# A hybrid decoder trunk on one core: a joined block merge, narrower state-space taps, parameters and a mask moved

## The chip, the cores and the metric

The kernel runs on one core of a Trainium2 chip. The metric is device time in microseconds (us) of one execution. Engines: TensorE (PE, matmuls; PEld is its weight load), VectorE (DVE), ScalarE (ACT), GpSimd (POOL), and SyncE (SP), whose queue issues all DMAs here.

## What is computed

Two layers over 512 tokens of width 1024, batch 1. Layer 0 mixes with gated DeltaNet heads (4 heads of 128, chunked) and dilated sliding-window attention (8 heads of 64); layer 1 with a diagonal complex state-space mixer (S5: 64 groups of 16 channels, 64 states). Each mixer is followed by cross attention into 256 memory tokens and a SwiGLU feed-forward part, with post-norm after each. The parts that the change touches, cut from the reference:

```python
decay = jnp.exp(jnp.where(causal, g[..., :, None] - g[..., None, :], -jnp.inf))
lower = jnp.where(strict, jnp.einsum('bhnid,bhnjd->bhnij', k_beta, k), 0.0) * decay
sol = lax.linalg.triangular_solve(lower + eye, rhs, left_side=True, lower=True, unit_diagonal=True)
...
a_bar = jnp.exp(a * dt)
b_bar = ((a_bar - 1.0) / a)[..., None] * lax.complex(b_re.astype(f32), b_im.astype(f32))
_, states = lax.associative_scan(_lin_rec_combine, (a_seq, bu), axis=1)
y = (jnp.einsum('ghp,bsgp->bsgh', c_re, states.real) - jnp.einsum('ghp,bsgp->bsgh', c_im, states.imag))
```

## The kernel before

**Work.** Large products are made of three matmuls on high and low halves: ACT rounds a loaded weight tile (`raw`) to `hi`, DVE subtracts to make `lo` (`_load`, lines 504 to 516), PE multiplies. There are two `raw` buffers and four each of `hi` and `lo`. Small products use f32 operands directly.

**Order.** The program isn't issued as written. Each call adds an operation to a list (`Order.add`); `Order.order` (line 283) then plays the list through with a cost for each operation and a latency between engines, and always gives a free engine the ready operation of lowest priority number. The number is the place in the program plus `bias`; weights come 200 places early, and `LATER` = 100 puts an operation 100 places later. Limits on tile buffers keep it from running far ahead. The result is a fixed order on each engine's queue. `together` puts several matmuls side by side as one planned operation. The cost function has no entry for loading an ACT function table.

**Stages.** `build` (line 1624): mixer 0, output projection and norm, values of the memory, cross attention (`xattn`), feed-forward part 0 with the state-space tables as fill, state-space mixer, its gated output, cross attention, feed-forward part 1.

**Mixer 0** (line 600). Constants come first: `upper`, `masks`, a 64 KB `level` mask and the 640 KB attention mask (lines 632 and 633, in one `big` tile), convolution weights and small parameters, then the weights of the beta and decay logits. After the key projection, 16 matmuls of the broadcast log decay `gl` with the triangular `upper` give every row's cumulated decay (line 770). For the triangular solve the unit lower blocks are inverted by levels. Sixteen (head, chunk) matrices of 128 hold four 32x32 blocks each; all 64 are inverted on DVE in 31 steps (two operations a step, line 826 on). Line 844 then adds `s5_params` to the list: small DVE operations on 128x32 tiles, with Sin and Tanh on ACT, that make `rot`, `rho4`, `cin`, `cout` for the tables. The gate projection z follows (line 853). The 32x32 inverses are laid out block-diagonally (`Xm`, and transposed in `TTs`), and each chunk is merged to 64x64 blocks (lines 867 to 883): the lower coupling is masked by `level`, and three products of four full 128x128x128 f32 matmuls follow; both copies are updated by a subtraction. The merge to 128 (lines 884 to 896) uses 64x64x64 matmuls on one quadrant. The recurrence over chunks, then the attention follow.

**Tables** (`s5_tables`, line 1327). For each of 8 blocks of 8 groups the taps are made: for q in 4, a matmul with a 128x128 stationary slice of `st` and a 32-column moving slice of `cb`, real and imaginary part accumulated (lines 1467 to 1470), one ACT copy, the skip weight on the diagonal, and copies into a banded matrix that is stored to DRAM (`s5m`) and read in the state-space stage. Every block is one step of the fill of feed-forward part 0, at `LATER`.

Of the kernel before, what the change touches and what calls it, by code (L numbers as in the profile page):

```python
# [12 lines left out]
AF = mybir.ActivationFunctionType  # L13
OP = mybir.AluOpType
AX = mybir.AxisListType

P = 128
# [3 lines left out]
NT = S // P  # L21
# [17 lines left out]
LATER = 100  # L39
# [416 lines left out]
def run(steps):  # L456
    for _ in steps:
        pass


class Trunk:
# [23 lines left out]
    def t2(self, dt=F32):  # L485
        return self.o.tile(self.tp, [P, 512], dt, self.nm("t2"), "t2", T2)
# [113 lines left out]
    def mixer0(self, fill):  # L600
        tc, nc, a = self.tc, self.nc, self.a
        V, A, G, T = self.o.V, self.o.A, self.o.G, self.o.T
        sb = self.cp
        t2, tiny = self.t2, self.tiny
        small = lambda w, name="s", dt=F32: sb.tile([P, w], dt, name=self.nm(name), bufs=1)
        w_in = a["hyb_w_in"][0]

        xTv, _, actf, actt = self.feat_view([self.big() for _ in range(4)])
# [14 lines left out]
        upper = small(P, "upper")  # L623
# [4 lines left out]
        ktok = self.big(F32).rearrange("p (t c) -> p t c", t=4)  # L628
        cb = self.big(F32)
        attm = cb[:, :1280]  # L630
        level = cb[:, 1280:1408]
        self.o.SP.dma_start(level, a["level"])
        self.o.SP.dma_start(attm, a["attmask"])
        convw = small(48, "convw")
        self.o.SP.dma_start(convw, a["conv_t"])
        prm = small(8, "prm")
# [69 lines left out]
        gl = small(16, "gl")  # L706
# [3 lines left out]
        gc = small(16, "gc")  # L710
# [50 lines left out]
        LTs, Ds = four(), four()  # L761
        hsl = lambda h: slice(h * P, (h + 1) * P)
        h4 = lambda x: x.rearrange("p (h c) -> p h c", h=4)
        bc4 = lambda m: m[:, None, :].to_broadcast([P, 4, P])
        for c in range(NT):
            gB = self.bank()
            Dc = Ds[:, c]
            for h in range(4):
                o = c * 4 + h
                T.matmul(gB[:, hsl(h)], gl[:, o:o + 1].to_broadcast([P, P]), upper, start=True, stop=True)  # L770
            for h in range(4):
                o = c * 4 + h
                V.scalar_tensor_tensor(Dc[:, hsl(h)], gB[:, hsl(h)], gc[:, o:o + 1], causal, op0=OP.subtract, op1=OP.min)
            A.activation(Dc, Dc, AF.Exp)
# [15 lines left out]
        for c in range(NT):  # L790
            ts = slice(c * P, (c + 1) * P)
            rB = self.bank()
            gr = self.bank()
            for h in range(4):
                o = c * 4 + h
# [3 lines left out]
            for h in range(4):  # L799
                o = c * 4 + h  # L800
# [8 lines left out]
        TTs = four()  # L809
# [24 lines left out]
        for c in range(NT):  # L834
            ts = slice(c * P, (c + 1) * P)
# [3 lines left out]
            for h in range(4):  # L839
                o = c * 4 + h  # L840
                Dh = Ds[:, c, hsl(h)]
                V.scalar_tensor_tensor(Dh, qk[:, hsl(h)], rk[:, o:o + 1], Dh, op0=OP.mult, op1=OP.mult)

        self.s5_params()


        def z_sink(tt, ps):
            th = t2()
# [1 line left out]
            V.scalar_tensor_tensor(th, th, 1.0, ps, op0=OP.add, op1=OP.mult)  # L850
            V.scalar_tensor_tensor(h4(zgt[:, tt]), h4(th), 0.5, bc4(normg), op0=OP.mult, op1=OP.mult)

        self.gemm_tok(w_in, 0, KT, 1536, actt, NT, z_sink, tail=TAIL)


# [2 lines left out]
        Xms = []  # L858
        for c in range(NT):
            self.o.SP.dma_start(Xc[:, c], s2v[c])  # L860
            Xm = t2()
            V.tensor_tensor(Xm.rearrange("p (h b i) -> p h b i", h=4, b=4), Xc[:, c, :, None, :].to_broadcast([P, 4, 4, 32]),
                            bm[:, None, :, None].to_broadcast([P, 4, 4, 32]), op=OP.mult)
            tp = self.transposes(lambda h: Xm[:, hsl(h)], 4)
            A.activation(TTs[:, c], tp, AF.Copy)
            Xms.append(Xm)
        for c in range(NT):
            XT, Xm = TTs[:, c], Xms[c]
            E = t2()
            V.tensor_tensor(h4(E), h4(LTs[:, c]), bc4(level), op=OP.mult)  # L870
            yp = self.bank()
            for h in range(4):
                T.matmul(yp[:, hsl(h)], E[:, hsl(h)], Xm[:, hsl(h)], start=True, stop=True)
            Y = t2()
            A.activation(Y, yp, AF.Copy)
            xp = self.bank()
            for h in range(4):
                T.matmul(xp[:, hsl(h)], XT[:, hsl(h)], Y[:, hsl(h)], start=True, stop=True)
            xtp = self.bank()
            for h in range(4):  # L880
                T.matmul(xtp[:, hsl(h)], Y[:, hsl(h)], XT[:, hsl(h)], start=True, stop=True)
            V.tensor_tensor(Xm, Xm, xp, op=OP.subtract)
            V.tensor_tensor(XT, XT, xtp, op=OP.subtract)
        lo_, up_ = slice(0, 64), slice(64, P)
        for c in range(NT):
            LT, XT, Xm = (h4(x) for x in (LTs[:, c], TTs[:, c], Xms[c]))
            yp = self.bank()
            for h in range(4):
                T.matmul(h4(yp)[up_, h, lo_], LT[lo_, h, up_], Xm[lo_, h, lo_], start=True, stop=True)
            Y = t2()  # L890
            A.activation(h4(Y)[up_, :, lo_], h4(yp)[up_, :, lo_], AF.Copy)
            xtp = self.bank()
            for h in range(4):
                T.matmul(h4(xtp)[lo_, h, up_], h4(Y)[up_, h, lo_], XT[up_, h, up_], start=True, stop=True)
            V.tensor_scalar(XT[lo_, :, up_], h4(xtp)[lo_, :, up_], -1.0, None, op0=OP.mult)
# [16 lines left out]
        for c in range(NT):  # L912
            ts = slice(c * P, (c + 1) * P)
            Dc, TT = Ds[:, c], TTs[:, c]
            vb = vbt[:, c]
            if c:
# [4 lines left out]
                for h in range(4):  # L921
                    o = c * 4 + h
                    V.scalar_tensor_tensor(r[:, hsl(h)], kS[:, hsl(h)], nrbg[:, o:o + 1], vb[:, hsl(h)],
                                           op0=OP.mult, op1=OP.add)
# [7 lines left out]
            if c < NT - 1:  # L932
# [4 lines left out]
                if c:  # L937
                    for h in range(4):
                        V.scalar_tensor_tensor(Sn[:, hsl(h)], St[:, hsl(h)], egl[:, c * 4 + h:c * 4 + h + 1], su[:, hsl(h)],
                                               op0=OP.mult, op1=OP.add)  # L940
# [6 lines left out]
            if c:  # L947
# [4 lines left out]
                for h in range(4):  # L952
                    V.scalar_tensor_tensor(o_[:, hsl(h)], qS[:, hsl(h)], eg[:, c * 4 + h:c * 4 + h + 1], o_[:, hsl(h)],
                                           op0=OP.mult, op1=OP.add)
# [17 lines left out]
            for h in range(4):  # L972
                V.scalar_tensor_tensor(om[:, hsl(h)], o_[:, hsl(h)], ms[:, h:h + 1], zgt[:, c, hsl(h)],
                                       op0=OP.mult, op1=OP.mult)
# [352 lines left out]
    def s5_tables(self):  # L1327

        a = self.a
        V, A, G, T = self.o.V, self.o.A, self.o.G, self.o.T  # L1330
# [71 lines left out]
        for b in range(8):  # L1402
# [6 lines left out]
            blk = lambda n: part(n).rearrange("p (q c) -> p q c", q=4)  # L1409
            st = [self.t2() for _ in range(2)]  # L1410
# [47 lines left out]
            for n in range(2):  # L1458
                tp = self.transposes(lambda k: st[n][:, k * P:(k + 1) * P], 4)
                A.activation(part(2 + n), tp, AF.Copy)  # L1460

            cb = self.t2()
            cbv = cb[:, :256].rearrange("p (n q g h) -> p n q g h", n=2, q=4, g=2)
            for n in range(2):
                V.tensor_tensor(cbv[:, n], C[n][:, qs, None, :].to_broadcast([P, 4, 2, 16]),
                                self.gmask[:, n, None, :, None].to_broadcast([P, 4, 2, 16]), op=OP.mult)
            tp = self.bank()
            for q in range(4):
                for n in range(2):
                    T.matmul(tp[:, q * 32:(q + 1) * 32], st[n][:, q * P:(q + 1) * P],  # L1470
                             cb[:, n * P + q * 32:n * P + q * 32 + 32], start=(n == 0), stop=(n == 1))
            ts = self.t2()
            tsv = ts[:, :P].rearrange("p (q c) -> p q c", q=4)
            A.activation(ts[:, :P], tp[:, :P], AF.Copy)
            di = ts[:, P:2 * P].rearrange("p (q c) -> p q c", q=4)
            V.tensor_tensor(di[96:], self.ident[96:, None, 96:].to_broadcast([32, 4, 32]),
# [2 lines left out]
            for d in range(4):  # L1479
                src = tsv[(3 - d) * 32:(4 - d) * 32]  # L1480
                for k in range(4 - d):
                    dst = blk(6)[k * 32:(k + 1) * 32, :, (k + d) * 32:(k + d + 1) * 32]
# [141 lines left out]
    def build(self):  # L1624
        self.setup()
        k = self.mem_k(0)
        self.mixer0(k)
        run(k)
        self.mix_out0()
        run(self.mem_v(0))  # L1630
        self.xattn(0)
        tables = self.s5_tables()
        self.hp, self.hp_open = [self.big(F32) for _ in range(2)], True
        self.ffn(0, None, tables)
        self.hp_open = False
        run(tables)
        kv = chain(self.mem_k(1), self.mem_v(1))
        for _ in range(PRE):
            next(kv)
        gtok = self.s5(kv)  # L1640
        self.glu(gtok)
        self.xattn(1)
        self.ffn(1, self.to_out())
        self.o.issue()
# [58 lines left out]
```

## Time and profile before

| | us |
|---|---|
| median of 3 runs | 1561.4 (1559.45 to 1561.63) |
| the profiled execution | 1559.76 |
| its span, first to last instruction | 1557.9 |
| PE busy | 1523.2 |
| DVE busy | 989.4 |
| ACT busy | 555.2 |

Nearly every instruction carries line 439, the helper that issues the planned list, so groups are told apart by tile and shape. `big`, `t`, `tiny`, `ps` stand for all tiles of a pool. A line of a timeline has the start, the time from start to end of the merged run, engine, line, operation, out<-in, shape, count, and in brackets the idle time before it with what ended it. An f32 matmul appears as two records, a transpose through PE as one.

### The profile page before, as it was taken

To read this page: it belongs to the slowest core of one execution; us is meant where nothing else is said; L and a number is where in the kernel's file an instruction comes from. 1 tells how busy PE (TensorE), PEld (TensorE's weight loads), DVE (VectorE), ACT (ScalarE), POOL (GpSimd) and SP (SyncE) were. 2 spreads that over 40 slices of the span, in tenths; PEclk is the share of its full clock that TensorE was granted. 3 is DMA by queue.
4 is the path that set the end of the run, shared out by engine and by line. 5 is a ranking of instruction groups with operands and counts; after the bars stand their busy time and mean duration, and the time that the engine had idled before them with its cause. 6 is when DMAs were issued, how large, how long until landed. Compare 5 with 4: busy or idle time off the path is not lost.

```text
span 1557.9 us, 20944 instructions
## 1 busy us (share of the span) xinstructions
PE 1523.2 (98%) x8132; PEld 1285.8 (83%) x8132; DVE 989.4 (64%) x1890; ACT 555.2 (36%) x996; POOL 57.6 (4%) x97
## 2 busy tenths in 40 slices
PE   7999999999999999999999899999999999999998
PEld 5887878689888888888888798888888888888886
DVE  6989666675657788635853899648647444234436
ACT  6533436624432343323441243323422332122311
POOL 1000000010100000010000000000000000000000
PEclk9999999999999999999999999999999999999999
DMA  6423224135213454436572553333212433233322
GB/s 180 123 70 96 82 81 136 60 99 154 81 62 115 122 187 143 172 117 196 196 234 86 213 174 136 115 114 103 75 55 82 122 96 95 82 108 105 98 68 95
DMA packets 125539, 184.06 MB, mean 118 GB/s; under 512 B 14144, under 2 KB 84800, under 8 KB 121344
## 3 DMA queue, kind: packets, MB, share of 16 engines
q1 hardware_dynamic: 125440, 182.73, 37.3%
q8 instruction: 64, 1.05, 0.3%
q14 instruction: 35, 0.29, 0.1%
HBM read 162.52 MB, written 20.19 MB: 117 GB/s over the span
## 4 chain that ended last, share of the span: by engine, by line
PE 84%; DVE 10%; DMA 2%; ACT 2%; issue 1%; SPq 0%; POOL 0%; DVEq 0%; ACTq 0%; POOLq 0%
PE ps L439 83%; DVE t L439 5%; DVE big L439 2%; DVE lo L439 2%; PE ps L437 1%; DMA raw<-in_xo_w_dram 1%; ACT big L439 1%; DVE tiny L439 1%; ACT hi L439 1%; DMA big<-s5m 0%; ACT L439 0%; DMA t<-in_x_t_dram 0%; DMA raw<-in_xv_w_dram 0%; DMA raw<-in_hyb_w_in_dram 0%; DMA prm<-in_dn_a_log_dram 0%
## 5 line engine op out<-in xcount | busy, mean ns | idle before, releaser
L439 PE MATMUL ps<-big,hi 128*128 128x512 f32 (+1 forms) x2368 | 648.3, 360 | 6.0 <-ACT hi L439 4.5
L439 PE MATMUL ps<-hi,big 128*128 128x512 f32 x1728 | 547.8, 394 | 0.7 <-ACT big L439 0.4
L439 PEld LDWEIGHTS ps<-big,hi 128*128 128x128 f32 x2368 | 419.8, 189 | 69.8 <-ACT hi L439 5.0
L439 ACT ACTIVATE hi<-raw 128x1024 fp32r<-128x1024 f32 (+2 forms) x252 | 263.4, 1046 | 517.5 <-PE ps L439 341.9
L439 DVE TENSOR_TENSOR lo<-raw,hi 128x1024 fp32r<-128x1024 f32 (+2 forms) x252 | 303.5, 1205 | 226.2 <-ACT hi L439 223.9
L439 PE MATMUL ps<-big,lo 128*128 128x512 f32 (+1 forms) x1184 | 424.1, 360 | 2.4 <-DVE lo L439 2.4
L439 PEld LDWEIGHTS ps<-hi,big 128*128 128x128 f32 x1728 | 322.5, 188 | 66.1 <-DVE big L439 0.9
L439 PE MATMUL ps<-lo,big 128*128 128x512 f32 x864 | 339.1, 394 | 4.2 <-DVE lo L439 3.9
L439 PEld LDWEIGHTS ps<-big,lo 128*128 128x128 f32 x1184 | 223.8, 189 | 34.0 <-DVE lo L439 3.0
L439 PEld LDWEIGHTS ps<-lo,big 128*128 128x128 f32 x864 | 162.4, 188 | 39.3 <-DVE lo L439 6.6
L439 ACT ACTIVATE big<-ps 128x256 fp32r<-128x256 f32 (+2 forms) x188 | 89.6, 508 | 205.8 <-PE ps L439 196.9
L439 ACT ACTIVATE t<-ps 128x512 f32<-128x512 f32 (+4 forms) x133 | 66.7, 512 | 155.7 <-PE ps L439 151.3
L439 DVE TENSOR_TENSOR big<-ps,big 128x256 fp32r<-128x256 f32 (+1 forms) x152 | 77.5, 541 | 54.6 <-ACT big L439 52.6
L439 DVE SCALAR_TENSOR_TENSOR big<-big,ps 128x512 f32<-128x512 f32 x56 | 38.3, 684 | 93.8 <-PE ps L439 93.8
L439 DVE SCALAR_TENSOR_TENSOR t<-t,ps 128x512 f32<-128x512 f32 x72 | 48.9, 681 | 56.7 <-ACT t L439 51.7
L439 ACT ACTIVATE big<-t 32x128 f32<-32x128 f32 (+2 forms) x148 | 64.4, 455 | 32.4 <-DVE t L439 14.2
L439 DVE SCALAR_TENSOR_TENSOR big<-big,tiny,t 128x512 f32<-128x512 f32 x96 | 66.5, 744 | 0.0
L439 PE MATMUL ps<-ident,t 128*128 128x128 f32 x336 | 61.1, 276 | 4.7 <-ACT t L439 3.0
L439 POOL TENSOR_TENSOR tiny<-tiny,mhalf 128x1 f32<-128x1 f32 (+1 forms) x28 | 23.6, 846 | 965.8 <-DVE tiny L439 965.8
L439 PEld LDWEIGHTS ps<-ident,t 128*128 128x128 f32 x336 | 41.8, 141 | 16.4 <-issue 5.6
L439 PE MATMUL ps<-big,big 128*128 128x256 f32 (+2 forms) x328 | 55.2, 314 | 0.0
L439 DVE TENSOR_TENSOR big<-t,big 128x512 fp32r<-128x512 f32 (+1 forms) x68 | 44.0, 680 | 13.9 <-ACT big L439 13.7
(144 smaller groups left out, 994.4 us busy)
## 6 DMA issues: line engine op xcount, KB each, us to landing
raw<-in_ffn_wg_dram SPq DMA_DIRECT2D x44, 512.0 KB, 3.6
raw<-in_ffn_wu_dram SPq DMA_DIRECT2D x44, 512.0 KB, 3.7
raw<-in_ffn_wd_dram SPq DMA_DIRECT2D x44, 512.0 KB, 3.8
s5m<-big SPq DMA_DIRECT2D x16, 1024.0 KB, 4.5
big<-s5m SPq DMA_DIRECT2D x16, 1024.0 KB, 5.1
raw<-in_hyb_w_in_dram SPq DMA_DIRECT2D x26, 512.0 KB, 3.6
raw<-in_xk_w_dram SPq DMA_DIRECT2D x16, 512.0 KB, 4.8
raw<-in_xv_w_dram SPq DMA_DIRECT2D x16, 512.0 KB, 3.8
```

The costliest lines, as they stand in the source:

```text
L437: op.inst = getattr(self.eng[e], f)(*a, **k)
L439: op.inst = getattr(self.eng[e], fn)(*args, **kw)
```

## The change

Five edits. (1) The `level` load goes, and the attention mask is fetched just ahead of the gate projection. (2) The rows of cumulated decay come from a transpose of the broadcast `gc` instead of a matmul with `upper`. (3) The merge from 32 to 64 works on the 32x32 blocks themselves, for all 16 matrices at once: three stages of 16 pairs, each pair one 32x32x32 matmul for either 64-row half, into one bank a stage, without the mask; the results are copied into place with the sign turned. (4) The taps' operands are exchanged: `cb` slices of 32 columns are stationary, `st` moves, the four q go to four column groups of one bank; the result is copied and transposed once. (5) `s5_params` is called between the memory values and the first cross attention, with `LATER`.

```diff
@@ mixer0
-        level = cb[:, 1280:1408]
-        self.o.SP.dma_start(level, a["level"])
-        self.o.SP.dma_start(attm, a["attmask"])
...
-                T.matmul(gB[:, hsl(h)], gl[:, o:o + 1].to_broadcast([P, P]), upper, start=True, stop=True)
+                T.transpose(gB[:, hsl(h)], gc[:, o:o + 1].to_broadcast([P, P]), self.ident)
...
-        self.s5_params()
...
+        self.o.SP.dma_start(attm, a["attmask"])
         self.gemm_tok(w_in, 0, KT, 1536, actt, NT, z_sink, tail=TAIL)
...
-        for c in range(NT):
-            XT, Xm = TTs[:, c], Xms[c]
-            E = t2()
-            V.tensor_tensor(h4(E), h4(LTs[:, c]), bc4(level), op=OP.mult)
-            yp = self.bank()
-            for h in range(4):
-                T.matmul(yp[:, hsl(h)], E[:, hsl(h)], Xm[:, hsl(h)], start=True, stop=True)
-            Y = t2()
-            A.activation(Y, yp, AF.Copy)
-            xp = self.bank()
-            for h in range(4):
-                T.matmul(xp[:, hsl(h)], XT[:, hsl(h)], Y[:, hsl(h)], start=True, stop=True)
-            xtp = self.bank()
-            for h in range(4):
-                T.matmul(xtp[:, hsl(h)], Y[:, hsl(h)], XT[:, hsl(h)], start=True, stop=True)
-            V.tensor_tensor(Xm, Xm, xp, op=OP.subtract)
-            V.tensor_tensor(XT, XT, xtp, op=OP.subtract)
+        blk = [(slice(g * 64, g * 64 + 32), slice(g * 64 + 32, g * 64 + 64)) for g in range(2)]
+        all_ = [(c, h) for c in range(NT) for h in range(4)]
+        at32 = lambda x, c, h: x[:, (c * 4 + h) * 32:(c * 4 + h + 1) * 32]
...
+        def small(dst, rows, lhs, rhs):
+            for c, h in all_:
+                self.o.together(0.06, [((at32(dst, c, h)[rows[g]], lhs(c, h, g), rhs(c, h, g)), dict(start=True, stop=True))
+                                       for g in range(2)])
+        yp = self.bank()
+        small(yp, [b for _, b in blk], lambda c, h, g: LT4[c][blk[g][0], h, blk[g][1]],
+              lambda c, h, g: Xm4[c][blk[g][0], h, blk[g][0]])
+        Y = t2()
+        for _, b in blk:
+            A.activation(Y[b], yp[b], AF.Copy)
+        xtp = self.bank()
+        small(xtp, [a_ for a_, _ in blk], lambda c, h, g: at32(Y, c, h)[blk[g][1]],
+              lambda c, h, g: XT4[c][blk[g][1], h, blk[g][1]])
+        xp = self.bank()
+        small(xp, [b for _, b in blk], lambda c, h, g: XT4[c][blk[g][1], h, blk[g][1]],
+              lambda c, h, g: at32(Y, c, h)[blk[g][1]])
...
+        for a_, b in blk:
+            V.tensor_scalar(TT5[a_, :, :, b], v16(xtp)[a_], -1.0, None, op0=OP.mult)
+            for c in range(NT):
+                A.activation(Xm4[c][b, :, a_], v16(xp)[b, c], AF.Copy, scale=-1.0)
@@ s5_tables
-            for q in range(4):
-                for n in range(2):
-                    T.matmul(tp[:, q * 32:(q + 1) * 32], st[n][:, q * P:(q + 1) * P],
-                             cb[:, n * P + q * 32:n * P + q * 32 + 32], start=(n == 0), stop=(n == 1))
+            self.o.together(0.5, [((tp[q * 32:(q + 1) * 32, :P], cb[:, n * P + q * 32:n * P + q * 32 + 32],
+                                    st[n][:, q * P:(q + 1) * P]), dict(start=(n == 0), stop=(n == 1)))
+                                  for n in range(2) for q in range(4)])
             ts = self.t2()
...
+            A.activation(ts[:, 2 * P:3 * P], tp[:, :P], AF.Copy)
+            tp = self.transposes(lambda k: ts[:, 2 * P:3 * P], 1)
             A.activation(ts[:, :P], tp[:, :P], AF.Copy)
@@ build
         run(self.mem_v(0))
+        self.o.bias = LATER
+        self.s5_params()
+        self.o.bias = 0
         self.xattn(0)
```

## Rows read from the trace of the kernel before

**Rows 1.** The page, part 1: busy us, share of the span, instructions, by engine

```profile
PE 1523.2 (98%) x8132; PEld 1285.8 (83%) x8132; DVE 989.4 (64%) x1890; ACT 555.2 (36%) x996; POOL 57.6 (4%) x97
```

**Rows 2.** Busy time by stretch: stretch, length, busy us of PE, PEld, DVE, ACT, POOL; PEclk, DMA, GB/s

```profile
560.00:600.00 40.00, 40.00 (x197) 33.17 (x195) 36.30 (x70) 16.03 (x29) 0.53 (x1) 1.00 0.52 171
...
123.30:137.40 14.10, 10.45 (x45) 7.80 (x44) 13.86 (x60) 4.40 (x9) 0.00 (x0) 1.00 0.30 79
...
380.00:425.00 45.00, 44.48 (x286) 39.98 (x286) 26.13 (x42) 19.56 (x42) 3.62 (x2) 1.00 0.28 85
```

**Rows 3.** Waits of PE, 100 to 140 us: total us, times, longest

```profile
PE ps L439 <- DVE lo L439: 3.6, 2, 3.1
```

**Rows 4.** DMA issues (KB each, us to landing) and the traffic of 11.9 to 19 us

```profile
big<-in_attmask_dram SPq DMA_DIRECT2D x1, 640.0 KB, 6.5
...
DMA packets 5022, 1.97 MB, mean 277 GB/s; under 512 B 3422, under 2 KB 4894, under 8 KB 5022
```

**Rows 5.** Timeline of ACT and of PE, first 40 us

```profile
18.88 0.69 ACT L439 ACTIVATE t<-ps,convw 128x512 f32<-128x512 f32 x1 [1.74 <-DMA convw<-in_conv_t_dram]
...
21.33 3.88 PE L439 MATMUL ps<-big,t 128*16 128x512 f32 x16 [1.46 <-DVE t L439]
...
37.36 0.66 PE L439 MATMUL ps<-ident,big 128*128 128x128 f32 x4 [2.82 <-DVE big L439]
```

**Rows 6.** Groups of PE over the whole span: count, busy us, mean ns, idle before

```profile
L439 PE MATMUL ps<-upper,gl 128*128 128x128 f32 x32 | 4.1, 277 | 0.0
...
L439 PE MATMUL ps<-ident,rb 128*128 128x128 f32 x16 | 2.2, 272 | 0.0
```

**Rows 7.** Timeline of DVE, 100 to 165 us: parameter operations and one low-half split

```profile
115.35 0.18 DVE L439 SCALAR_TENSOR_TENSOR tiny<-tiny,tiny 128x32 f32<-128x32 f32 x1
...
132.11 1.21 DVE L439 TENSOR_TENSOR lo<-raw,hi 128x1024 fp32r<-128x1024 f32 x1
...
139.32 0.49 DVE L439 TENSOR_TENSOR tiny<-pw 128x32 f32<-128x32 f32 x4
...
143.10 0.20 DVE L439 TENSOR_TENSOR cin<-tiny 128x32 f32<-128x32 f32 x1
```

**Rows 8.** Timeline of ACT: function table loads behind 100 us

```profile
124.54 1.28 ACT L439 ACT_TABLE_LOAD   x1
...
239.49 1.28 ACT L439 ACT_TABLE_LOAD   x1
```

**Rows 9.** Timeline of PE in the merges, 148 to 157 us

```profile
149.29 1.06 PE L439 MATMUL ps<-t,big 128*128 128x128 f32 x8
150.19 1.06 PE L439 MATMUL ps<-big,t 128*128 128x128 f32 x8
...
152.31 0.68 PE L439 MATMUL ps<-t,big 64*64 64x64 f32 x8
152.91 0.50 PE L439 MATMUL ps<-hi,big 128*128 128x512 f32 x1
...
156.31 0.27 PE L439 MATMUL ps<-t,big 64*64 64x64 f32 x1
...
156.53 0.34 PE L439 MATMUL ps<-t,big 64*64 64x64 f32 x3
```

**Rows 10.** Timeline of PE, taps of one block, feed-forward stage

```profile
554.09 1.64 PE L439 MATMUL ps<-t,t 128*128 128x32 f32 x14
555.57 0.48 PE L439 MATMUL ps<-big,lo 128*128 128x512 f32 x1
```

**Rows 11.** Timeline of PE, attention: pairs on two column groups, and what follows

```profile
266.09 0.66 PE L437 MATMUL ps<-t,big 128*64 128x128 f32 x8
266.68 0.39 PE L439 MATMUL ps<-big,hi 128*128 128x256 f32 x1
...
300.12 1.09 PE L437 MATMUL ps<-t,big 128*64 128x128 f32 x16
301.14 0.66 PE L439 MATMUL ps<-ident,t 128*128 128x128 f32 x4
```

More of the change, by code (lines that the diff above doesn't have):

```diff
@@ new lines, in mixer0 @@
+        all_ = [(c, h) for c in range(NT) for h in range(4)]
+        at32 = lambda x, c, h: x[:, (c * 4 + h) * 32:(c * 4 + h + 1) * 32]
+        LT4, XT4, Xm4 = ([h4(x[c]) for c in range(NT)] for x in ([LTs[:, c] for c in range(NT)], [TTs[:, c] for c in range(NT)], Xms))
+        def small(dst, rows, lhs, rhs):
+            for c, h in all_:
+                self.o.together(0.06, [((at32(dst, c, h)[rows[g]], lhs(c, h, g), rhs(c, h, g)), dict(start=True, stop=True))
+                                       for g in range(2)])
@@ L884, in mixer0 @@
+        v16 = lambda x: x.rearrange("p (c h k) -> p c h k", c=4, h=4)
+        TT5 = TTs.rearrange("p c (h i) -> p c h i", h=4)
+        for a_, b in blk:
+            V.tensor_scalar(TT5[a_, :, :, b], v16(xtp)[a_], -1.0, None, op0=OP.mult)
+            for c in range(NT):
+                A.activation(Xm4[c][b, :, a_], v16(xp)[b, c], AF.Copy, scale=-1.0)
         lo_, up_ = slice(0, 64), slice(64, P)
```

## The prediction

> **What bounds the kernel now.** I began with the page's busy shares: TensorE (PE) is busy in 1523.2 us of a span of 1557.9 us, VectorE (DVE) in 64% of it, ScalarE (ACT) in 36% [rows 1]. So PE time is the currency: an instruction taken off PE is worth its issue interval, wherever PE has other work to put there. The table by stretches says where that holds [rows 2]. In the feed-forward stage (560 to 600 us) PE is busy 40.00 of 40 us; in the cross attention (380 to 425 us) 44.48 of 45; at 123.3 to 137.4 us, where the 32x32 blocks are inverted on DVE, only 10.45 of 14.1, with DVE at 13.86. There PE waited 3.6 us in two waits for the low halves of weights, which DVE makes [rows 3]. Busy time of a matmul is not its price, as records overlap; I take prices from the distance between starts. An f32 matmul shows as two records, a transpose as one.
>
> **Start: two mask loads leave the first 16 us.** The mask is 640 KB [rows 4], the level mask 128x128 f32, 64 KB: 0.72 MB. In the stretch around them DMA moved 277 GB/s [rows 4], so what is queued behind them lands up to 2.6 us earlier. ACT then waited 1.74 us for the convolution weights, PE 1.46 us for the split weights of the beta and decay logits, loaded in the same burst, and 2.82 us more at 37 us [rows 5]. The first PE wait should go: **1.5 us**. The last stands behind DVE work and ACT's table loads, so I leave it. Ends: 0 and 4.3. Put later, the 640 KB take 2.4 us on the transfer engines at that rate; behind it on SP's queue stand weight loads of the gate projection, and the mask is read only in the attention. Cost nothing while PE holds queued weights, 2.4 if it doesn't.
>
> **Decay rows.** 16 f32 matmuls (32 records, 4.1 us) become 16 transposes like those of rb (16 records, 2.2 us) [rows 6]: **1.9 us**. They wait for gc, a small DVE copy, instead of gl; PE has projection matmuls meanwhile. Ends 1 and 2.
>
> **Parameters out of the inversion.** By the code s5_params is 102 DVE operations beside two memsets that run at the start, 6 on ACT and 3 small DMAs. On DVE they ran one by one among the inversion's steps from 115.35 to 143.10 us, about 0.10 us each (four took 0.49 us, one 0.18) [rows 7], 10.5 us in all. About 35 of them, 3.7 us, stand before the low-half split at 132.11 us, on which PE's 3.1 us wait ended [rows 3]; a second wait of 0.5 us follows from the same queue. Without them both should go: 3.6 us, of which I take **3.4**, since that split also needs its raw load, which is late next. Ends 1.5 and 3.65. The split of the following weights and the inversion itself come earlier too; I count nothing for it, as PE is busy there.
> In the cross attention the same 10.5 us lie on a DVE with 18.9 us free in 45 [rows 2], at a priority 100 places back. Queued behind each is at most a maximum, reciprocal or split that PE reads; with 0.10 us a piece a late one costs little. On ACT the sine functions need another table: before, one load at 124.54 us and one back at 239.49 us, 1.28 us each [rows 8]; both should go there and come back between the exponentials. I charge **0.7 us**; ends 0 and 5.1 (four loads uncovered).
>
> **Merge 32 to 64.** Before, each of four chunks has three times four f32 matmuls of 128x128x128: 96 records, 8 in 0.90 us [rows 9], so 0.112 each, 10.8 us. After, 96 matmuls of 32x32x32 in pairs on two row groups, 192 records. The nearest rows are the 64x64x64 matmuls of the next level: alone, 8 records take 0.60 us [rows 9]; where two row groups run together (156.31 to 156.53, six starts in 0.22 us), 0.037 each. A 32-wide matmul streams half as long, so the pitch may fall to 0.018; I take the middle, 0.027, 5.2 us, plus an entry of 0.15 (worked out under the taps) at each of three stages: 5.7, a saving of **5.0 us**. Ends: 0.018 saves 6.8; the lone pitch of 0.075 makes 14.4 us, a loss of 3.6. I stay by the paired rows, since the new ones are issued in pairs too.
> The Trainium skill, "TensorE: Matmul & The Clock Gate", section "Wait — 56ns, not 53.3ns?", speaks against the merge: about 62 ns per matmul where its instructions are decoded in microcode, else a floor of about 25 ns; 192 records would be an estimated 11.9 us or 4.8. The six starts 0.037 us apart speak for the second.
> On DVE twelve 128x512 operations go, two small ones come; on ACT four copies become two and eight short ones. The new chain is joined: all of a stage, then two ACT copies, then the next. A 128x512 ACT operation takes 0.69 us [rows 5], so PE without cover would stand about 2.8 us over two such pauses; cover is the value projection's matmuls, whose weights DVE can now split earlier. Cost nothing.
>
> **Taps.** Each of 8 blocks issues 16 records of 128x32, 14 of them in 1.48 us [rows 10]: 1.8 us with the entry. After, 16 records in four column groups of 32. The attention's pairs of 64 columns show the price of two groups: 8 records took 0.59 us, 16 took 1.02 [rows 11], so 0.055 each and 0.15 once, half the whole-array pitch. Four groups would give 0.028 if they all overlap, 0.055 if only two do: 0.45 to 0.88 us, I take 0.65; plus 0.15 and one transpose of 0.14 [rows 6]. 1.8 less 0.9 is 0.9 a block, **7.2 us**; ends 4 and 9.5. The extra ACT copy and the later chain end in a store that nothing in this stage reads; hidden by the stage's matmuls, without that cover one short ACT copy a block, under 0.69 us [rows 5]. The stage is PE's entirely [rows 2], so nothing but PE can eat the gain.
> The Trainium skill, "TensorEngine Tiling (Array Packing)", section "Key Properties", says that changing the tiling mode drains the engine. The trace agrees: 0.15 us a visit, eight visits 1.2 us, which the 7.2 above already hold.
>
> **Sum.** 1.5 + 1.9 + 3.4 - 0.7 + 5.0 + 7.2 = 18.3 us. The profiled execution took 1559.76 us (span 1557.9); it would be 1541.5. The median of the runs is 1561.4, 1.6 above it, so **1543 us**. The ends sum to a gain of -4.6 (0 + 1 + 1.5 - 5.1 + 4 - 3.6 - 2.4) and 26; all at once is unlikely. A measurement can tell 0.2% (3.1 us) from no change.
>
> **Rivals.** (a) Small matmuls are bound by issue and don't overlap: the merge loses 3.6, the taps gain 5.1 (0.055 a record); sum 1.5 + 1.9 + 3.4 - 0.7 - 3.6 + 5.1 = 7.6, **1554 us**. For it: no row shows a 32x32 matmul; against: the six starts [rows 9]. Chance 0.17. The 62 ns of the Trainium skill above are a milder form of this case.
> (b) In the mixer another chain (recurrence, attention) ends last, and what PE saves there turns into waits: only taps and parameter cost stay, 6.5 us, **1555 us**. For it: DVE at 13.86 of 14.1 [rows 2]; against: PE still has work in nearly every stretch. Chance 0.11.
> (c) Slower: the planner's costs know no table load. If each of the 6 parameter functions on ACT falls alone between exponentials, that is 12 loads of 1.28 us, 15.4 us; with 10.5 us on DVE before the softmax, 25.9 us against 19.0 saved elsewhere: **1568 us**. It decides once more than 19 of the 25.9 are uncovered. Against: ACT has 25 us free in 45, DVE 19 [rows 2]. Chance 0.05.
> (d) The change doesn't do what it says: the planner only orders by priority, and may run the parameters before the cross attention, beside the output projection's norms. The gain stays, the 0.7 may be 2: **1544 us**. Chance 0.05.
>
> **Numbers.** The forecast holds 0.62 and spans 1533 to 1551 by itself (sizes of merge, taps and start). To leave out no more than 2 in 10 the range must take in most of (a) and (b): 1533 to 1556. Faster by over 0.2%: the forecast, (d), and most of (a) and (b), 0.90; within 0.2%: 0.05; slower: 0.05.
>
> **What would show it.** Right: no PE wait on a low half near 130 us; PE waits before 40 us shorter by the 1.46; taps at about 0.8 us of PE per block with its transpose; the merge's 192 records in under 7 us; two table loads moved behind 300 us, with no new PE wait there over 0.5 us; PE busy time down by about 15 us. Wrong: merge records 0.06 us apart or more, taps of 1.1 us or more, PE idle growing at 140 to 200 us or in the cross attention.

## The result, and the profile after

The changed kernel takes 1542.71 us (median; 1541.12 to 1543.56), a ratio of 0.988 (95% interval 0.9868 to 0.9893) to the kernel before. Measured a second time, beside other runs, the ratio was 0.9894 (0.9879 to 0.9908). 1543 us was forecast. The sum holds, but not term by term: the gains for the start and the decay rows do not show in the time, and taps, merge and parameters brought more than they were given.

The page's first part, after [rows 1]:

```profile
PE 1508.7 (98%) x8220; PEld 1268.3 (82%) x8220; DVE 984.9 (64%) x1880; ACT 552.5 (36%) x1008; POOL 57.0 (4%) x97
```

The span is 1541.8 us, 16.1 less; PE is busy 14.5 us less. So, taken together, 1.6 us came from shorter waits and the rest from PE work that is gone. Where the waits went shows by stretches; columns as in [rows 2], the first four lines after, the last before:

```profile
120.00:160.00 40.00, 39.93 (x410) 33.08 (x409) 22.86 (x45) 13.70 (x26) 0.00 (x0) 1.00 0.44 119
160.00:200.00 40.00, 34.52 (x214) 29.75 (x213) 24.72 (x82) 17.79 (x55) 4.39 (x4) 0.96 0.15 53
320.00:360.00 40.00, 39.53 (x198) 32.95 (x196) 37.68 (x102) 18.54 (x33) 4.80 (x5) 1.00 0.42 122
560.00:600.00 40.00, 40.00 (x212) 32.00 (x211) 32.75 (x64) 20.81 (x43) 1.10 (x3) 1.00 0.58 197
```
```profile
160.00:200.00 40.00, 38.83 (x279) 34.00 (x278) 26.52 (x88) 19.93 (x60) 4.03 (x4) 1.00 0.24 79
```

The 3.6 us of [rows 3] are gone: in 120 to 160 us PE lacks 0.07 us. But in the next 40 us it lacks 5.48, at a granted clock of 0.96; before, it was busy there for 38.83 of 40. A wait near 130 us went and new ones came some 40 to 50 us later. The timeline of PE, after, answers to [rows 5, 6, 9, 10]:

```profile
19.13 3.87 PE L439 MATMUL ps<-big,t 128*16 128x512 f32 x16 [1.02 <-DVE t L439]
26.78 1.05 PE L439 MATMUL ps<-masks,t 16*128 16x8 f32 x8 [2.42 <-DVE t L439]
...
50.53 0.60 PE L439 MATMUL ps<-ident,gc 128*128 128x128 f32 x4
...
58.45 0.60 PE L439 MATMUL ps<-ident,rb 128*128 128x128 f32 x4
...
144.77 0.69 PE L437 MATMUL ps<-t,big 32*32 32x32 f32 x32
145.39 1.09 PE L439 MATMUL ps<-ident,t 128*128 128x128 f32 x8
146.41 0.69 PE L437 MATMUL ps<-t,big 32*32 32x32 f32 x32
147.04 0.50 PE L439 MATMUL ps<-lo,big 128*128 128x512 f32 x1
...
149.78 1.10 PE L437 MATMUL ps<-big,t 32*32 32x32 f32 x58
150.70 0.22 PE L437 MATMUL ps<-t,big 32*32 32x32 f32 x2
...
151.83 0.50 PE L439 MATMUL ps<-hi,big 128*128 128x512 f32 x1
...
170.10 1.13 PE L439 MATMUL ps<-t,big 128*128 128x128 f32 x8 [0.77 <-DVE big L439]
...
171.53 0.40 PE L439 MATMUL ps<-hi,big 128*128 128x512 f32 x1
...
178.84 1.02 PE L439 MATMUL ps<-ident,t 128*128 128x128 f32 x4 [0.72 <-DVE t L439]
182.20 5.44 PE L439 MATMUL ps<-t,big 128*128 128x128 f32 x32 [2.34 <-DVE big L439]
187.47 0.60 PE L439 MATMUL ps<-ident,t 128*128 128x128 f32 x4
...
563.51 0.40 PE L439 MATMUL ps<-big,lo 128*128 128x512 f32 x1
563.84 0.64 PE L437 MATMUL ps<-t,t 128*32 128x128 f32 x16
564.41 0.73 PE L439 MATMUL ps<-big,hi 128*128 128x512 f32 x2
```

Read by starts. Merge: 58 records from 149.78 to 150.70, 0.016 us each; the first stage takes 0.62 and 0.63 us for 32 records each, the last two, 128 records, take 2.05 us to 151.83. Taps: 16 records in 0.57 us, with entry and transpose some 0.8 us a block. Recurrence: between the projection matmuls at 171.53 and 187.83 us none stands among its steps, six waits from 169 us on add up to 5.5 us, and behind the last of them 32 records take 5.27 us, 0.165 each instead of 0.112. The granted clock of that stretch is 0.68, as the mean of a part at half clock and a part at full (same columns):

```profile
182.20:187.47 5.27, 5.27 (x32) 5.27 (x33) 4.79 (x15) 3.55 (x12) 0.00 (x0) 0.68 0.00 0
```

Why PE has nothing to fill in shows on ACT, whose three copies at 183.79 us (and one at 185.99) are those of the value projection, finished on PE by some 143.8 us. In the kernel before they run nearly as late (last line):

```profile
183.79 1.57 ACT L439 ACTIVATE big<-ps 128x512 f32<-128x512 f32 x3 [2.85 <-PE ps L439]
...
185.99 0.59 ACT L439 ACTIVATE big<-ps 128x512 f32<-128x512 f32 x1
```
```profile
181.72 1.57 ACT L439 ACTIVATE big<-ps 128x512 f32<-128x512 f32 x3 [1.45 <-PE ps L439]
```

They write a `big` tile, of which the kernel has 16. By the planned order all are taken until the recurrence gives one back; two are held from the start by constants for the tables, writes without any input, which the planner placed at once (DVE and POOL, after; the same in the kernel before):

```profile
0.98 0.25 DVE L439 MEMSET big<- 128x32 f32 x4
```
```profile
1.72 1.81 POOL L439 MEMSET big<- 128x2048 f32 x1
```

Until then four of the eight PSUM banks (the buffers that matmuls write) hold the value projection, two more the first rotary tiles, and the planner has two left for the recurrence. No view of the trace shows which buffer is taken: this is read from the code and its plan, and e4, e9 and e12 test it.

The mask, finally, was hardly fetched later. It was issued at 14.60 us (11.95 before): nothing comes before it, so the planner gave it to SP as soon as SP was free. The weight load behind it landed late, and ACT waited 4.04 us at 22.51.

```profile
14.60 2.09 SPq L439 DMA_DIRECT2D big<-in_attmask_dram  x1
```
```profile
22.51 1.06 ACT L439 ACTIVATE hi<-raw 128x1024 fp32r<-128x1024 f32 x1 [4.04 <-DMA raw<-in_hyb_w_in_dram]
```

### The profile page after: what moved, and what is told of

Same layout as the page of the kernel before. It is cut to its first block, busy times and chain, and to the rows that moved or that the text cites. A ratio compares the mean times of both kernels' runs of the same rounds, so it can differ in the third digit from the quotient of the medians.

```text
span 1541.8 us, 21120 instructions
## 1 busy us (share of the span) xinstructions
PE 1508.7 (98%) x8220; PEld 1268.3 (82%) x8220; DVE 984.9 (64%) x1880; ACT 552.5 (36%) x1008; POOL 57.0 (4%) x97
## 3 DMA queue, kind: packets, MB, share of 16 engines
q8 instruction: 65, 1.06, 0.3%
## 4 chain that ended last, share of the span: by engine, by line
PE 88%; DVE 7%; DMA 2%; ACT 1%; issue 1%; SPq 0%; POOL 0%; DVEq 0%; ACTq 0%; POOLq 0%
PE ps L439 86%; DVE t L439 4%; DVE big L439 2%; PE ps L437 2%; DVE lo L439 1%; DMA raw<-in_hyb_w_in_dram 1%; DVE tiny L439 0%; DMA big<-s5m 0%; ACT big L439 0%; DMA raw<-in_xo_w_dram 0%; ACT hi L439 0%; ACT t L439 0%; DMA posi<-in_pos_t_dram 0%; SPq L439 0%; ACT L439 0%
## 5 line engine op out<-in xcount | busy, mean ns | idle before, releaser
L439 ACT ACTIVATE t<-ps 128x512 f32<-128x512 f32 (+6 forms) x147 | 68.8, 485 | 147.7 <-PE ps L439 139.0
L439 PEld LDWEIGHTS ps<-big,big 128*128 128x128 f32 x328 | 47.8, 190 | 5.0
```

The source lines that it names most:

```text
L439: op.inst = getattr(self.eng[e], fn)(*args, **kw)
```

## The experiments

Each ratio is to the kernel before on the same chip; e1 to e4, e5 to e8, e9 to e11 and e12 are four groups, so runs of different groups are compared by their ratios. 0.001 is 1.6 us. Where the changed kernel did not run beside them, its two ratios' mean, 0.9887, is the base; a difference of two ratios is uncertain by about 0.0018, 2.8 us.

| run | median us | ratio (95%) |
|---|---|---|
| e1_old_taps | 1551.66 | 0.994 (0.9928 to 0.9952) |
| e2_old_merge | 1549.73 | 0.9928 (0.9915 to 0.994) |
| e3_params_back | 1548.91 | 0.9918 (0.9904 to 0.9931) |
| e4_buffers_free | 1545.24 | 0.9876 (0.9854 to 0.9898) |
| e5_changed_again | 1545.11 | 0.9894 (0.9879 to 0.9908) |
| e6_mask_late | 1546.59 | 0.9917 (0.9891 to 0.9944) |
| e7_old_decay | 1544.05 | 0.9891 (0.9877 to 0.9904) |
| e8_params_later | 1545.05 | 0.9894 (0.9881 to 0.9907) |
| e9_x_later | 1534.50 | 0.9821 (0.9808 to 0.9835) |
| e10_x_later_two_halves | 1535.77 | 0.983 (0.9817 to 0.9844) |
| e11_x_later_old_merge | 1542.26 | 0.9874 (0.9859 to 0.9888) |
| e12_before_buffers_free | 1560.01 | 0.9991 (0.9981 to 1.0) |

### One part undone

**e1: the old taps.**

```diff
-            A.activation(ts[:, 2 * P:3 * P], tp[:, :P], AF.Copy)
-            tp = self.transposes(lambda k: ts[:, 2 * P:3 * P], 1)
...
+                    T.matmul(tp[:, q * 32:(q + 1) * 32], st[n][:, q * P:(q + 1) * P],
+                             cb[:, n * P + q * 32:n * P + q * 32 + 32], start=(n == 0), stop=(n == 1))
```

> The changed kernel with the old order of the taps' operands (128-column slices of st stationary, 32 columns moving, no second copy, no transpose); the rest of the change stays. My theory (PE issue time is the whole price of the taps, about 1.0 us a block by the trace of the changed kernel): the gain over the kernel before shrinks by 7 to 8.5 us, so 1550.5 us against 1542.7, all of the difference between the starts of the first and the last weight load of the feed-forward part. Rival (the feed-forward part has another bound, and the gain there came from the planner's new order): less than 3 us, 1545 us.

0.0053 slower than the base, 8.3 us: the theory's upper end. The stage itself says it more closely. Its stores of the banded matrix, two a block (start of the first and of the last; after, then e1), span 236.7 us after and 243.7 in e1: 7.0 us over seven blocks, 1.0 us a block, as much as PE's records are longer. PE's issue time is the whole price of the taps.

```profile
L439 SPq DMA_DIRECT2D s5m<-big x16: 338/339/339, 540.2 to 776.9; - x16
L439 SPq DMA_DIRECT2D s5m<-big x16: 338/339/459, 541.7 to 785.4; - x16
```

**e2: the old merge.**

```diff
+        self.o.SP.dma_start(level, a["level"])
         self.o.SP.dma_start(attm, a["attmask"])
...
+            V.tensor_tensor(h4(E), h4(LTs[:, c]), bc4(level), op=OP.mult)
...
+            V.tensor_tensor(Xm, Xm, xp, op=OP.subtract)
+            V.tensor_tensor(XT, XT, xtp, op=OP.subtract)
```

> The changed kernel with the old merge from 32 to 64, chunk by chunk with 128x128x128 products and the level mask (its 64 KB load stands beside the attention mask's); the rest of the change stays. Theory A (the merge saves 7 us of PE, but the recurrence behind it became the bound, with 4.3 us of new PE waits and half clock between 169 and 188 us): PE is busy about 7 us longer, the waits at 170 to 184 us shrink by 3 to 4 us, and the time grows by only 2 to 4 us, 1545 to 1547 us. Theory B (the waits belong to the recurrence whatever the merge is): the time grows by the whole 7 us, 1550 us, and the waits stay.

0.0041, 6.4 us, uncertain by 2.8: by the time nearer to B, and the waits stay, as B says. So the merge did not make the new stall, and keeps most of what its records save, some 7 us. The waits of PE, e2, 160 to 200 us (total, times, longest):

```profile
PE ps L439 <- DVE big L439: 3.1, 2, 2.3
PE ps L439 <- DVE t L439: 1.5, 3, 0.7
```

**e3: the parameters among the inversion's steps.**

```diff
+        self.s5_params()
         def z_sink(tt, ps):
...
         run(self.mem_v(0))
-        self.o.bias = LATER
-        self.s5_params()
-        self.o.bias = 0
```

> The changed kernel with the state-space parameters made among the inversion's steps again; the rest of the change stays. Theory A (the parameters delay the low-half splits at 130 us by 3.6 us, and their place beside the output projection's norms costs 1 us): PE's wait for a low half near 130 us is back with 3 to 3.6 us, and the time grows by 1.5 to 2.7 us, 1544 to 1545.5 us. Theory B (the recurrence bounds the mixer, and the inversion is its start, so the 3.6 us come later to all of it): the time grows by 3.5 us or more, 1546 us and up. Theory C (what was gained at 130 us is lost again at 170 us): no difference over 0.7 us.

0.0031, 4.8 us, uncertain by 2.8: the size fits B, but A's upper end too, and B's mechanism is not what the trace shows, as the recurrence's stall is gone (PE busy 38.23 of 40 at 160 to 200 us). The wait near 130 us comes back larger than before, 5.44 us for 3.6. PE reaches it no earlier, at 130.57 us (130.25 before); but the split that it needs starts at 134.75 us instead of 132.11 [rows 7], after DVE had waited 0.71 and 1.04 us for ACT's parameter functions. Behind it the clock falls, to 0.50 at 137 to 140 us. PE's and DVE's timeline and PE's stretch (stretch, length, PE busy, clock, DMA, GB/s), e3:

```profile
136.01 0.79 PE L439 MATMUL ps<-lo,big 128*128 128x512 f32 x1 [5.44 <-DVE lo L439]
```
```profile
130.14 0.20 DVE L439 TENSOR_TENSOR pw<-t 128x32 f32<-128x32 f32 x1 [1.04 <-ACT t L439]
...
134.75 1.21 DVE L439 TENSOR_TENSOR lo<-raw,hi 128x1024 fp32r<-128x1024 f32 x1
```
```profile
120.00:140.00 20.00, 14.56 (x56) 0.86 0.23 61
```

So in these three kernels (before, after, e3) the two stalls exclude each other: PE pauses either for the low half at 130 us or, if not there, in the recurrence at 170 us.

**e7: the old decay rows**, beside **e5**, the changed kernel again.

```diff
-                T.transpose(gB[:, hsl(h)], gc[:, o:o + 1].to_broadcast([P, P]), self.ident)
+                T.matmul(gB[:, hsl(h)], gl[:, o:o + 1].to_broadcast([P, P]), upper, start=True, stop=True)
```

> The changed kernel itself, as the base for the three runs beside it: the ratio to the kernel before should be 0.988 again, within 0.001.

> The changed kernel with the rows of cumulated decay made by f32 matmuls of gl with the triangular matrix again (32 records for 16). Theory A (PE is full there, so what the records cost is what the time gives): 1.5 to 2 us slower, 1544.5 us. Theory B (the chain gl, gc, transpose is longer than gl, matmul, and that cost is given back): no difference over 0.7 us.

0.9891 against 0.9894: no difference that the runs can tell. They can't rule theory A out, as its 1.5 to 2 us are less than their uncertainty of 2.8. e5 lies just outside what was expected.

### Parts moved

**e6: the mask really late.**

```diff
+        V.tensor_copy(attm[:, :1], LTs[:, 3, :1])
         self.o.SP.dma_start(attm, a["attmask"])
```

> The changed kernel with a true order for the attention mask: one small DVE copy of a value of the last chunk's lower triangle into the mask's tile stands ahead of the load, so that the load can't start before some 100 us; in the changed kernel it was issued at 14.60 us. Theory A (the mask's 640 KB at the start still delay a weight load, on which ACT waited 4.04 us and PE 2.42): PE's waits before 40 us shrink by 1 to 2.5 us and the time falls by as much, 1540 to 1542 us. Theory B (those waits hang on the decay's chain of small DVE operations and on ACT's table loads): no difference over 0.7 us.

Theory B, and nothing gained. The load now stands at 72.90 us and ACT's wait for a weight shrank from 4.04 to 1.44 us, but PE waits before 40 us as long as before [rows 5], now 1.19 and 3.84 us, on DVE:

```profile
19.80 3.89 PE L439 MATMUL ps<-big,t 128*16 128x512 f32 x16 [1.19 <-DVE t L439]
32.45 0.66 PE L439 MATMUL ps<-ident,big 128*128 128x128 f32 x4 [3.84 <-DVE big L439]
```

Its executions spread from 1543.51 us (mean granted clock 0.997) to 1557.14 (0.987). Four of the six, 1543.51 to 1546.69, are like those of e5 (1543.85 to 1545.97); the other two lost some 10 us. The profiled one, 1554.3 us, is of these, and shows where: PE stands for 0.47 us with nothing that the profile shows to wait for ("issue") among the last records of the merge, and the next 14 us run at a clock of 0.51 (columns as in [rows 2]). e4 has more on this.

```profile
152.74 0.31 PE L437 MATMUL ps<-t,big 32*32 32x32 f32 x7 [0.47 <-issue]
```
```profile
153.00:167.00 14.00, 14.00 (x86) 10.90 (x84) 3.21 (x6) 4.68 (x14) 0.00 (x0) 0.51 0.26 76
```

**e8: the parameters later.**

```diff
-        self.o.bias = LATER
-        self.s5_params()
-        self.o.bias = 0
         self.xattn(0)
+        self.s5_params()
```

> The changed kernel with the state-space parameters called after the cross attention instead of before it, so that they run in its second half (about 390 to 410 us) and not beside the output projection's norms (300 to 363 us). Theory A (their place costs about 1 us where DVE is at 37.7 of 40 us): 0.5 to 1.5 us faster, PE waits at 320 to 360 us gone. Theory B (the sine functions now fall between exponentials, with table loads of 1.28 us each): four to eight table loads between 380 and 420 us and 1 to 4 us slower. Theory C (both are hidden): no difference over 0.7 us.

0.9894 as e5: theory C, as far as the runs can tell (A's 0.5 to 1.5 us would be hidden, but A's waits did not go). DVE has 133 operations at 400 to 440 us instead of 33, and two table loads, at 404.49 and 414.95 us, among the exponentials; PE's waits at 300 to 440 us go from 1.0 to 1.7 us.

### The new stall

**e4: buffers free.** The tables' first writes get an input that is late, and the loads of x, which fill two more `big` tiles, wait for the value projection's last copy, so that they don't take what comes free. The two were not tried apart.

```diff
-            V.memset(d[0][:, :, 0:1], 1.0)
-            V.memset(d[1][:, :, 0:1], 0.0)
+            for n in range(2):
+                V.tensor_scalar(d[n][:, :, 0:1], rot[n], 0.0, 1.0 - n, op0=OP.mult, op1=OP.add)
...
+            V.tensor_scalar(blks[1][:, :32], self.rho4, 0.0, None, op0=OP.mult)
             G.memset(blks[1], 0.0)
...
+        self.late = Vt[:, 3, :1]
...
+            self.o.V.tensor_copy(self.h[k][:, :1], self.late)
             self.o.SP.dma_start(self.h[k], xv[k])
```

> The changed kernel with two sets of writes made later: the first writes into the tables' big tiles (constants that depend on nothing and so were placed at the start, from where they hold two of the 16 big buffers all through the mixer) now come after the state-space parameters, and the residual's loads of x come after the value projection's copies. Nothing else is changed. Theory A (between 169 and 188 us PE has nothing to put between the recurrence's steps because four banks hold the value projection's results, whose copies wait for a big buffer): with a buffer free the copies come near 140 us, projection matmuls fill the recurrence, PE's waits between 169 and 184 us (about 5 us with the half clock behind them 7) go, and the time falls by 4 to 6 us, to 1537 to 1539 us. Theory B (the recurrence's own chain of latencies on DVE and ACT bounds that stretch): the waits move but the end of the recurrence stays, less than 1 us gained.

The waits went as A says (PE busy 38.82 of 40 at 160 to 200 us), the time hardly fell. Its five executions took 1538.15, 1539.64, 1545.24, 1545.96 and 1547.5 us, at mean granted clocks of 0.996, 0.997, 0.993, 0.992 and 0.991: two at or near the forecast, three slower by some 7 us, at a lower clock. The profiled one, the slowest, shows where. PE's timeline, e4:

```profile
150.58 0.86 PE L437 MATMUL ps<-t,big 32*32 32x32 f32 x43
153.12 0.44 PE L437 MATMUL ps<-t,big 32*32 32x32 f32 x16 [1.69 <-issue]
```

In the middle of one stage of the merge PE stood for 1.69 us on "issue", as in e6. The transfers of 150 to 151.5 us, just ahead of the pause, by queue (packets, MB, share of 16 engines):

```profile
q1 hardware_dynamic: 239, 0.48, 84.2%
q8 instruction: 1, 0.02, 3.9%
```

One packet of instructions, 0.02 MB, took 0.94 us (3.9% of 16 engines over 1.5 us) beside weights and x at 333 GB/s. I read it as PE's next instructions coming late, and set e9 to test it; but the rows show a coincidence and no more, and two other traces speak against the traffic. In e6 the loads of x come at 197.00 us, the stretch of 150 to 151.5 us moves 51 GB/s, nothing is transferred in the next 1.5 us, and the pause is there all the same; its packet took 1.06 us (4.4%). In e9 one at 151.5 to 153 us took 1.03 us (4.3%), without any pause. Behind the pause in e4 PE is full and at half clock (stretch, length, PE busy, clock, DMA, GB/s):

```profile
140.00:153.00 13.00, 11.43 (x219) 1.00 0.71 209
153.00:167.00 14.00, 13.88 (x106) 0.53 0.09 34
```

14 us at 0.53 are 6.6 us of work not done, about the loss seen.

**e9: the loads of x behind the last rotary projection.**

```diff
-        self.late = Vt[:, 3, :1]
+        self.late = qkT[0][:, 3, 511:512]
```

> As e4_buffers_free, but the residual's four loads of x (2 MB) come after the last rotary projection instead of after the value projection's copies, so that they don't run beside the joined merge. Theory A (in e4 an instruction fetch of PE queued behind that traffic, and the pause of 1.69 us among the 32x32 matmuls and 13 us at half clock behind it cost about 7 us in three of five executions): no such pause, full clock from 145 to 180 us, and 1537 to 1540 us in all executions. Theory B (the half clock comes from the small matmuls themselves): half clock there in the profile, executions spread over 1538 to 1547 us again. Theory C (the buffers don't matter): 1543 to 1545 us.

Better than A: 1534.5 us (1531.98 to 1535.24), 0.0066 under the base, some 10 us, uncertain by 2.8. It beats both kernels. No pause, full clock, and the recurrence filled (PE busy 38.37 of 40 at 160 to 200 us). A's cause for the pause is not shown by it: four executions without one fit A, but e6 has a pause without that traffic, and in e4 itself two of five executions lost nothing. e9, same columns:

```profile
140.00:153.00 13.00, 13.00 (x240) 1.00 0.50 132
153.00:167.00 14.00, 14.00 (x146) 1.00 0.10 35
```

The value projection's first copy now runs at 130.74 us. How long the recurrence lasts shows between the first and the last start of one DVE operation (count, shortest, median and longest ns, first and last start); in the kernel before, after, and e9:

```profile
L439 DVE SCALAR_TENSOR_TENSOR t<-ps,nrbg,big x12: 343/343/352, 170.1 to 187.7; 128x128 f32<-128x128 f32 x12
```
```profile
L439 DVE SCALAR_TENSOR_TENSOR t<-ps,nrbg,big x12: 340/343/351, 163.0 to 187.9; 128x128 f32<-128x128 f32 x12
```
```profile
L439 DVE SCALAR_TENSOR_TENSOR t<-ps,nrbg,big x12: 329/342/351, 161.6 to 178.8; 128x128 f32<-128x128 f32 x12
```

17.6 us, 24.9, 17.2. The change started the recurrence 7 us earlier and ended it at the same time; with buffers it also ends 9 us earlier. The first store of the banded matrix stands at 531.8 us in e9, 540.2 after and 542.7 in e5, so the gain is there before the tables. Why e9 is also 3.6 us under e4's best execution is not shown; they ran on different chips, and the loads of x have another place.

**e10: e9 with the merge in two halves**, each with banks and a `Y` of its own.

```diff
+        for cs in ((0, 1), (2, 3)):
...
+            small(yp, [b for _, b in blk], lambda c, h, g: LT4[c][blk[g][0], h, blk[g][1]],
+                  lambda c, h, g: Xm4[c][blk[g][0], h, blk[g][0]], cs)
```

> As e9_x_later, with the joined merge cut in two: all three stages for chunks 0 and 1, then for chunks 2 and 3, so that no more than 64 of the 32x32 records stand together and projection matmuls can come between. Theory A (joining all 16 matrices costs nothing): within 1 us of e9. Theory B (192 records close together bring the half clock or the pause): 2 to 6 us faster than e9, if e9 shows them. Theory C (the more numerous short copies, and two visits more, cost): 0.5 to 1.5 us slower.

0.983 to 0.9821, 1.4 us slower and within the uncertainty: B falls, A and C can't be told apart. Cut in two the merge is no faster, so joining all 16 matrices costs nothing that shows.

**e11: e9 with e2's edit.**

> As e9_x_later, with the old merge of 128x128x128 products. Theory A (the merge is worth the 7 us of PE that it saves, with free buffers too): 6 to 8 us slower than e9, 1544 to 1547 us. Theory B (the dense small matmuls cost clock behind them, which free buffers lay open): 0 to 4 us slower than e9, and full clock from 145 to 190 us.

Theory A: 0.0053 slower than e9, 8.3 us; the 6.4 of e2 lie within the uncertainty.

**e12: the kernel before, with e9's edit.** The tables' writes wait for the output projection's norm, as `rho4` comes too early there.

```diff
         self.mix_out0()
+        self.late1 = self.const([P, 1], name='late1')
+        self.o.V.tensor_copy(self.late1, self.h[0][:, :1])
...
+            V.tensor_scalar(blks[1][:, :32], self.late1.to_broadcast([P, 32]), 0.0, None, op0=OP.mult)
             G.memset(blks[1], 0.0)
```

> The kernel before with the edit of e9_x_later alone: the first writes into the tables' big tiles wait for the output projection's norm, the residual's loads of x for the last rotary projection. Theory A (the shortage of big buffers bounds the recurrence in the kernel before as well, independent of the change): 6 to 9 us faster than the kernel before, 1552.5 to 1555.5 us. Theory B (before, the recurrence starts later behind the inversion's stall and the long merge, and PE has projection matmuls left for it, so that the change laid the shortage open): less than 3 us, 1558.5 us or more, with PE busy at 160 to 200 us as it was, 38.8 of 40 us.

Theory B: 0.9991. The buffers are free, as the value projection's copies begin at 152.65 us instead of 181.72, but PE is busy 38.75 of 40 us at 160 to 200 us, as before, and the recurrence takes the same 17.7 us (172.2 to 189.9). e12, stretch and ACT:

```profile
160.00:200.00 40.00, 38.75 (x293) 34.59 (x292) 25.36 (x84) 18.26 (x56) 4.03 (x4) 1.00 0.09 27
```
```profile
152.65 0.60 ACT L439 ACTIVATE big<-ps 128x512 f32<-128x512 f32 x1
```

The shortage cost nothing until the change took PE's pause at 130 us away; e3 says the same from the other side.

## Why the prediction was right, and where not

**Taps, 7.2: right, a little small.** 8 us by the stage's length (1.0 a block), 8.3 by e1. Four column groups overlap better than the 0.65 I took: 0.57 us for 16 records; the entry is about 0.1.

**Merge, 5.0: mechanism right, size off.** The mis-sized term is the pitch, 0.027 "as the middle"; it is 0.016, under the lower end of 0.018. All 192 records take 3.3 us by starts, and some 3.8 with an estimated 0.5 for three entries (the transposes ahead of the first two take 0.97 and 1.02 us to the next start, 0.79 elsewhere), instead of 5.7. So about 7 us are saved on PE, and 6.4 (e2) to 8.3 us (e11) in time. The floor of about 25 ns from one start to the next that the Trainium skill gives ("TensorE: Matmul & The Clock Gate", section "Wait — 56ns, not 53.3ns?") does not bind here: 58 starts in 0.92 us, in pairs on two row groups.

**Joined chain at no cost: right.** PE lacks 0.07 us in 120 to 160, and cutting the chain in two gives nothing (e10).

**Parameters, 3.4 less 0.7: both waits went, and the place was rival (d).** They ran at 300 to 363 us beside the output projection's norms, with table loads at 312.60 and 384.88 us, and cost one wait of 0.5 us there; e8 shows that the place hardly matters. Undoing them costs 4.8 us against the 2.7; the two agree within the uncertainty, and e3's plan also puts the split 2.6 us later than before, so that PE waits 5.44 us and the clock falls behind it.

**Start, 1.5: wrong.** The step that failed is "two mask loads leave the first 16 us": the code moved the mask, the planner did not, as nothing comes before it. The next step, that the PE wait hangs on those loads, fell in e6: with the mask at 72.90 us PE waits 5.0 us before 40 us (without the 4.4 until the first weights), against 3.4 in the changed kernel, 4.7 in e5 and 5.2 before. The first row of the decay's transposes on PE stands at 50.53 us after, 52.96 in e5, 50.91 for the matmuls before: no gain. And the granted clock is lower there: 0.91 (0.83 in e5) at 20 to 40 us against 1.00 before. That is not shown to be the change's doing, as e12, whose start is that of the kernel before, has 0.88 there.

**Decay, 1.9: there on PE, not in the time.** From that row to the last of rb PE needs 7.92 us instead of 9.61, 1.7 less. But with the matmuls put back (e7) the same stretch takes 8.58, and no time is lost that the runs can tell; 1.9 us is less than they can.

**What the sum left out: rival (b), in part.** "I count nothing for it, as PE is busy there", of all that comes earlier behind 140 us, is the step that failed: the recurrence became the bound of its stretch, with 5.5 us of waits and a clock of 0.68 behind them. e9, which frees the buffers, is some 10 us faster; 160 to 200 us place 5.5 of these (3.9 of PE's waits, 1.6 of clock), where the rest lies is open. The text named the sign (PE idle growing at 140 to 200 us) and gave it 0.11 as a whole; it came beside the gains, not in their place. Terms by the runs are 8.3 + 6.4 + 4.8, 19.5 us for the parts undone one at a time (which need not add up), against 17.6 by the base. Taps, merge and parameters were forecast at 14.9 together, 4.6 too small; start and decay at 3.4, of which nothing shows. These errors nearly cancel, so the forecast's closeness is partly luck.

## What to carry to other kernels

Where a planner or scheduler places the work, look what each moved operation waits for: one without inputs goes to the front wherever it is written, and a constant written early holds its buffer from there on. When a stall goes, ask which buffers the work behind it will need at the new time, not only which engine is busy. Small matmuls on separate row or column groups can be far cheaper than the whole-array pitch, so size them by their narrowest overlapping rows.

## What was not expected of the hardware

f32 matmuls of 32x32 in pairs on two row groups issue at 0.016 us a record. Twice PE stood in the midst of them without a wait that the profile shows: for 1.69 us in e4, as data moved at 333 GB/s just ahead, and for 0.47 us in e6, where it was 51. Behind either pause the granted clock stayed near 0.5 for 14 us (0.53 and 0.51) although PE was busy in 13.88 and 14.00 of them. In the changed kernel, in e9 and in e10 the same records ran through at 1.00. What makes the pause, and why some executions take such a dip and others of the same kernel do not, is open.
